# Taking the gathered rows of u at an even pace, earlier, with a higher claim on VectorE

## The chip, the cores and the metric

One core of a Trainium2 chip runs the whole program. The metric is the device time of one execution in microseconds (us). Before the change the median of three runs is 2525.91 us (2525.65 to 2526.83).

## The reference, cut to what matters

Two transformer blocks over 512 tokens of width 1024. The change touches only the last part of the second block, a mixture of 16384 tiny experts (`peer`):

```python
q = (h @ w_pq)...                       # 8 heads, two halves of the key
sc = einsum("bshcd,hcnd->bshcn", q, sub_keys)
s_top, i_top = lax.top_k(sc, 16)        # best 16 of 128 sub-keys, per half
cand = s_top[..., 0, :, None] + s_top[..., 1, None, :]
best, pos = lax.top_k(cand, 16)         # best 16 of 256 pairs
expert_idx = ...                        # 8 x 16 = 128 experts per token
gate = softmax(best)
a = gelu(einsum("ced,cd->ce", u_emb[idx], hx))
out = einsum("ce,ced->cd", gate * a, v_emb[idx])
```

Each token needs 128 rows of `u_emb` (a dot product with the token's h) and 128 rows of `v_emb` (a weighted sum), each row 1024 floats.

## The kernel before, in words

**Two ways for the experts.** The 512 tokens lie in four blocks of 128. Tokens of blocks 1 to 3 (384) are computed densely: h times all 16384 columns of u on TensorE, then times a gate matrix that is zero for experts not chosen, then times all of v. Tokens of block 0 are computed by gathering: for each of their 128 expert slots an indirect DMA fetches one row of u per token into a 128 x 1024 tile (row n of the 128 u rows), and VectorE multiplies it with h and sums (`tensor_tensor_reduce`, in the profile `CUSTOM_DVE_ANT_0`) into column n of `ea`. After all 128, the 128 rows of v follow, each added to `yt` with its weight. This makes 256 row steps (`row_step`, `rows[0]` counts them). Their gathers are issued from GpSimd's queue (L1045). There are four row buffers (`NROW`), `row0`, `row1` and the ends of two larger tiles, which the profile calls `last`; the gather into a buffer waits until VectorE is done with the row in it.

**The stages.** (1) `peer_u` computes the queries and the heads' lists of best sub-keys (`head_lists`). (2) It computes the dense u products in 16 octets of 8; each of these 128 `linear` calls is 24 matmuls of 128 x 384. Beside them run the routing of each block (`block_best`: best pairs, expert numbers, softmax; almost all on VectorE) and then `gates`, which builds the gate matrices: for each group of 8 tokens VectorE makes five `hot` tiles, and TensorE multiplies them in 24 small bf16 matmuls (`gp`). The results go to DRAM (`g_dr`), as do 14 of the 16 octets of activations (`a_dr`). (3) The last stage runs 128 steps (`for i in range(NV - NLAST)` and its end): per step VectorE multiplies activation and gate (`wv`), ScalarE and VectorE split it into a high and a low part, and TensorE does 24 matmuls (`acc`). Every eight steps the next octet of gates (`goct`) and of activations comes back from DRAM, 1.5 MB each.

**Weights** of u and v stream in as pairs of units (`feed`, `raw`); each unit is split into a high part by ScalarE (`w..h`) and a low part (`w..l`) by VectorE or, while `gates_on` is false in the u products, by GpSimd. The split runs two units ahead of its use.

**The order of the work** is written by a planner at build time, and each engine then runs its instructions in that order. `Clock` holds a planned time for each engine: `Clock.cost` prices a VectorE instruction at 0.07 us and a nanosecond or so per element, a matmul at (at least 256) columns / 2400 us. `Merge` runs a main generator, here `peer_u`, and beside it side generators in lanes (`ls` for lists, routing and gates, one after the other; `rw` for rows). Each side generator yields when it wants to go on; whenever the main one yields, every side generator whose time is not past TensorE's planned time goes on, the smallest time first, and with equal times the one started first. A yield of `room("V", slack)` means: VectorE's planned time less `slack`, so a generator with a larger slack may pile more work on VectorE ahead of TensorE and goes first. `block_best` uses 1.5, the hots of `gates` 2.0, and the gate matmuls wait until 2.5 us (`GLAG`) after their hots. `u_rows`, the generator of the change, is started at the end of block 0's routing. It ends when 128 rows are done; what it hasn't done by the end of `peer_u` is done in the last stage, where `quota` spreads all rows that are left over the steps.

Of the kernel before, what the change touches and what calls it, by code (L numbers as in the profile page):

```python
# [41 lines left out]
TD = T - P  # L42
NTC = TD // TC
WAHEAD = 2
NRES = 2
VORD = list(range(NOCT - 1, NOCT - 1 - NRES, -1)) + list(range(NOCT - NRES))

# [15 lines left out]
class Clock:  # L63
# [53 lines left out]
    def room(self, kind, slack, *aps):  # L117

        return lambda: max(self.free[kind] - slack, self.at(*aps) if aps else 0.0)
# [70 lines left out]
def body(tc, a):  # L190
    nc = tc.nc
    clk = Clock()
    V, S, G, PE = (Engine(clk, k, e) for k, e in (("V", nc.vector), ("S", nc.scalar), ("G", nc.gpsimd),
                                                  ("PE", nc.tensor)))
    at, room = clk.at, clk.room
    with ExitStack() as ctx:
# [841 lines left out]
        def row_buf(n):  # L1038
            return bufs_[n % NROW]

        def fetch_row(upto):
            while fetched[0] < min(upto, 2 * P):
                n = fetched[0]
                t = a["vn"] if n >= P else a["un"]
                nc.gpsimd.indirect_dma_start(row_buf(n), None, t,  # L1045
                                             bass.IndirectOffsetOnAxis(ap=eid[:, n % P:n % P + 1], axis=0))
                start = max(clk.free["G"], at(row_buf(n), eid))
                clk.free["G"] = start + 1.2
                clk.put(row_buf(n), start + 5.0)
                fetched[0] += 1  # L1050

        rows = [0]

        def row_step():


            n = rows[0]
            rows[0] += 1
            fetch_row(n + NROW)
            r, e = row_buf(n), ea[:, n % P:n % P + 1]  # L1060
            if n < P:
                V.tensor_tensor_reduce(r, r, h2t[0], 1.0, 0.0, ALU.mult, ALU.add, e)
            elif n == P:
                V.tensor_scalar(yts[0], r, e, None, ALU.mult)
            else:
                V.scalar_tensor_tensor(yts[0], r, e, yts[0], ALU.mult, ALU.add)
            if n == P - 1:
                S.activation(ea, ea, AF.Gelu)
                V.tensor_tensor(ea, ea, eg, ALU.mult)

        def u_rows():
            while rows[0] < P:
                fetch_row(rows[0] + NROW)
                yield room("V", 0.3, row_buf(rows[0]))
                row_step()
        iota = wk.tile([P, P], F32, name="iota")
        G.iota(iota, pattern=[[1, P]], base=0, channel_multiplier=0, allow_small_or_imprecise_dtypes=True)
        iota2 = wk.tile([P, P, 2], BF16, name="iota2")
# [50 lines left out]
        def block_best(b):  # L1129
# [48 lines left out]
            if b == 0:  # L1178
                V.scalar_tensor_tensor(eid, IJG[:, 0, 0], float(P), IJG[:, 0, 1], ALU.mult, ALU.add)
                V.tensor_copy(eg, IJG[:, 0, 2])  # L1180
                mg.spawn("rw", u_rows())
            yield room("V", 1.5)

        g_dr = dr.tile([NOCT, P, NTC, 8, TC], F32, name="g_dr")
        a_dr = [dr.tile([P, 8, TD], F32, name=f"a_dr{o}") for o in range(NOCT - NRES)]

# [59 lines left out]
        def peer_u():  # L1246
# [24 lines left out]
            for o in range(NOCT):  # L1271
                ao = acts[o % 2]
                if o >= NOCT - NRES:
                    aocts[o] = ao
                for j in range(8):
# [3 lines left out]
                    if o == NOCT - 1 and j == 7:  # L1279
                        for i in range(WAHEAD):  # L1280
                            list(weighted(i))
                    r = yield from linear(h2, f"u{o}{j}")
                    S.activation(ao[:, j], r[:, P:], AF.Gelu)
                if o < NOCT - NRES:
                    nc.scalar.dma_start(a_dr[o], ao)
# [31 lines left out]
        def weighted(i):  # L1317

            n, j = divmod(i, 8)
            ao, go = aocts[VORD[n]], octs[n]  # L1320
            w, h, l = t2(f"wv{i}"), t2(f"wv{i}h", F32R), t2(f"wv{i}l", F32R)
            d = slice(P, T)
            V.tensor_tensor(w[:, d].rearrange("p (c t) -> p c t", c=NTC),
                            ao[:, j].rearrange("p (c t) -> p c t", c=NTC), go[:, :, j, :], ALU.mult)
            S.activation(h[:, d], w[:, d], AF.Copy)
            yield
            V.tensor_tensor(l[:, d], w[:, d], h[:, d].bitcast(F32), ALU.subtract)
            if i == 0:
                S.activation(l[:, :P], ident, AF.Copy, scale=0.0)
            if j == 7:  # L1330
                del octs[n]
            ready[i] = h, l
# [9 lines left out]
        def mix(m, q, first, last):  # L1342

            wh, wl, vh, vl = q
            c = slice(m * P, (m + 1) * P)
            d = slice(P, T)
            e = slice(0, T) if first else d
            PE.matmul(acc8[m][:, e], vh[:, c], wl[:, e], start=first, stop=False)
            PE.matmul(acc8[m][:, d], vl[:, c], wh[:, d], start=False, stop=False)
            PE.matmul(acc8[m][:, d], vh[:, c], wh[:, d], start=False, stop=last)  # L1350
# [4 lines left out]
        for i in range(NV - NLAST):  # L1355
# [4 lines left out]
            quota = min(2 * P, row0 + 4 + i * (2 * P - row0) // (NV - 12))  # L1360
            w = weighted(i + WAHEAD)
            next(w)
# [6 lines left out]
            for m in range(KT):  # L1369
                mix(m, q, i == 0, False)  # L1370
        for i in range(NV - NLAST + WAHEAD, NV):
            list(weighted(i))
# [150 lines left out]
```

## Time and profile before

| | |
|---|---|
| median of three runs | 2525.91 us |
| profiled execution | 2525.12 us, its span 2523.4 us |
| TensorE (PE) busy | 2404.9 us, 95% |
| VectorE (DVE) busy | 1774.1 us, 70% |
| ScalarE (ACT) busy | 1022.2 us, 41% |
| GpSimd (POOL) busy | 747.6 us, 30% |
| DMA | 466.13 MB, mean 185 GB/s |
| mean granted clock of TensorE | 0.978 |

Busy times come from the hardware profiler and can overlap between engines. A wait names the engine or transfer that released it. A busy TensorE is not TensorE at its peak. Times in the tables count from the span's start.

### The profile page before, as it was taken

To read this page: it belongs to the slowest core of one execution; us is meant where nothing else is said; L and a number is where in the kernel's file an instruction comes from. 1 tells how busy PE (TensorE), PEld (TensorE's weight loads), DVE (VectorE), ACT (ScalarE), POOL (GpSimd) and SP (SyncE) were. 2 spreads that over 40 slices of the span, in tenths; PEclk is the share of its full clock that TensorE was granted. 3 is DMA by queue.
4 is the path that set the end of the run, shared out by engine and by line. 5 is a ranking of instruction groups with operands and counts; after the bars stand their busy time and mean duration, and the time that the engine had idled before them with its cause. 6 is when DMAs were issued, how large, how long until landed. Compare 5 with 4: busy or idle time off the path is not lost.

```text
span 2523.4 us, 33808 instructions
## 1 busy us (share of the span) xinstructions
PE 2404.9 (95%) x13113; PEld 2135.8 (85%) x13121; DVE 1774.1 (70%) x3172; ACT 1022.2 (41%) x1558; POOL 747.6 (30%) x581
## 2 busy tenths in 40 slices
PE   9999999999999999999999999999998988898987
PEld 7777888888776668888899999999998988898887
DVE  4647644433468888556799999975577878787885
ACT  4454423322355665533233457653332323232333
POOL 2122011100137767003252300022234434444431
PEclk9999999999999999999999999999999999899998
DMA  4110222222211112222245568888889998999982
GB/s 164 57 51 34 105 100 85 99 101 100 84 51 51 51 51 100 85 99 92 91 155 189 184 219 266 270 303 300 305 305 373 331 368 334 371 337 361 358 322 90
DMA packets 128896, 466.13 MB, mean 185 GB/s; under 512 B 9184, under 2 KB 60512, under 8 KB 95200
## 3 DMA queue, kind: packets, MB, share of 16 engines
q1 hardware_dynamic: 39456, 281.04, 30.4%
q0 software_dynamic: 36864, 134.23, 14.7%
q10 hardware_dynamic: 52416, 48.70, 5.8%
q8 instruction: 103, 1.69, 0.3%
q14 instruction: 57, 0.47, 0.1%
HBM read 414.65 MB, written 49.28 MB: 184 GB/s over the span
## 4 chain that ended last, share of the span: by engine, by line
PE 44%; issue 25%; DVE 11%; DMA 10%; POOL 7%; ACT 3%; POOLq 0%; DVEq 0%; SPq 0%; ACTq 0%
PE u L133 8%; PE up L133 5%; DMA last<-in_vn,eid 5%; PE gate L133 5%; DMA row<-in_vn,eid 4%; PE pq L133 3%; POOL last L1045 3%; POOL row L1045 3%; PE acc L133 2%; PE wo L133 2%; DVE yt L133 2%; PE qkb L133 2%; PE ao L133 2%; PE gc L133 2%; PE co L133 2%
## 5 line engine op out<-in xcount | busy, mean ns | idle before, releaser
L133 POOL TENSOR_TENSOR cy<-cy,cvt 128x511 f32<-128x511 f32 (+14 forms) x120 | 170.7, 1422 | 59.2 <-ACT cvt L133 42.9
L1045 POOL DMA_INDIRECT last<-in_un,eid x64 | 74.0, 1156 | 342.2 <-DVE ea L133 317.4
L133 ACT ACTIVATE last<-u 128x384 f32<-128x384 f32 x128 | 63.4, 495 | 251.8 <-PE u L133 251.6
L1045 POOL DMA_INDIRECT last<-in_vn,eid x64 | 88.8, 1388 | 103.4 <-DVE yt L133 95.3
L1045 POOL DMA_INDIRECT row<-in_vn,eid x64 | 87.1, 1360 | 106.5 <-DVE yt L133 96.1
L1045 POOL DMA_INDIRECT row<-in_un,eid x64 | 75.7, 1183 | 123.4 <-DVE ea L133 120.7
L133 ACT ACTIVATE stage<-gp 128x512 f32<-128x512 f32 x96 | 95.9, 1106 | 36.7 <-PE gp L133 20.4
L133 DVE SCALAR_TENSOR_TENSOR yt<-row,ea,yt 128x1024 f32<-128x1024 f32 x64 | 82.1, 1283 | 37.1 <-DMA row<-in_vn,eid 37.1
L133 DVE SCALAR_TENSOR_TENSOR yt<-last,ea,yt 128x1024 f32<-128x1024 f32 x63 | 80.8, 1283 | 38.1 <-DMA last<-in_vn,eid 38.0
L133 DVE TENSOR_TENSOR hot<-hot,ijb 128x1024 bf16<-128x1024 bf16 x144 | 91.4, 687 | 1.6
L133 DVE SCALAR_TENSOR_TENSOR cyp<-u,par,cyp 128x511 f32<-128x511 f32 (+28 forms) x116 | 85.4, 736 | 2.4
L133 ACT ACTIVATE cvt<-u,par 128x511 f32<-128x511 f32 (+14 forms) x120 | 78.6, 701 | 0.7 <-DVE u L133 0.7
L133 PEld LDWEIGHTS <-hot 128*128 128x128 bf16 x1152 | 66.4, 97 | 13.1 <-DVE hot L133 8.5
L133 PE MATMUL gp<-hot,hot 128*128 128x128 bf16 x1152 | 74.7, 219 | 2.7 <-DVE hot L133 2.6
L133 DVE TENSOR_TENSOR wv<-last,goct 128x384 f32<-128x384 f32 x128 | 70.9, 554 | 0.0
L133 DVE TENSOR_TENSOR hot<-iota,ijb 128x1024 bf16<-128x1024 bf16 x96 | 61.8, 686 | 0.1
L133 DVE CUSTOM_DVE_ANT_0 last<-last,h2s 128x1024 f32<-128x1024 f32 x34 | 41.6, 1223 | 23.8 <-DMA last<-in_un,eid 23.8
L133 DVE CUSTOM_DVE_ANT_0 row<-row,h2s 128x1024 f32<-128x1024 f32 x36 | 44.0, 1223 | 12.5 <-DMA row<-in_un,eid 12.5
L133 DVE TENSOR_TENSOR su<-up,n2r 128x512 f32<-128x512 f32 x22 | 15.2, 691 | 51.7 <-PE up L133 51.7
L133 DVE MAX8 stop__8676<-skc 128x8 f32<-128x128 f32 x128 | 36.8, 287 | 5.5 <-ACT skc L133 3.2
L133 PEld LDWEIGHTS o<-v,pT 128*128 128x128 f32 x224 | 27.8, 191 | 14.8 <-ACT pT L133 7.6
L133 DVE CUSTOM_DVE_ANT_0 last<-last,h2tok 128x1024 f32<-128x1024 f32 x30 | 36.5, 1216 | 5.1 <-DMA last<-in_un,eid 5.1
(6461 smaller groups left out, 8606.2 us busy)
## 6 DMA issues: line engine op xcount, KB each, us to landing
raw<-in_w SPq DMA_DIRECT2D x89, 1024.0 KB, 4.8
raw<-in_u SPq DMA_DIRECT2D x64, 1024.0 KB, 6.4
raw<-in_v SPq DMA_DIRECT2D x64, 1024.0 KB, 7.7
g_dr<-stage ACTq DMA_DIRECT2D x24, 1024.0 KB, 7.0
goct<-g_dr SPq DMA_DIRECT2D x16, 1536.0 KB, 12.5
a_dr<-last ACTq DMA_DIRECT2D x14, 1536.0 KB, 10.0
last<-a_dr SPq DMA_DIRECT2D x14, 1536.0 KB, 17.3
xT<-in_x_t SPq DMA_DIRECT2D x1, 1024.0 KB, 9.5
```

Source lines behind the costliest of these rows:

```text
L133: return f(*args, **kw)
L1045: nc.gpsimd.indirect_dma_start(row_buf(n), None, t, bass.IndirectOffsetOnAxis(ap=eid[:, n % P:n % P + 1], axis=0))
```

## The change

`u_rows` asks for VectorE with a slack of 1.5 us instead of 0.3, and after each row it yields a time `due`, 3.5 us of planned time after the one before (`PACE`), so that rows come evenly. If it falls behind, it may be at most two paces late, and then catches up. The gather of the row four ahead, which was issued right after a row step, is now issued when the next row is due.

```diff
+PACE = 3.5
...
         def u_rows():
+
+            due = clk.free["PE"]
             while rows[0] < P:
                 fetch_row(rows[0] + NROW)
-                yield room("V", 0.3, row_buf(rows[0]))
+                yield room("V", 1.5, row_buf(rows[0]))
+                due = max(due + PACE, clk.free["PE"] - 2 * PACE)
                 row_step()
+                yield due
```

## Rows read from the trace of the kernel before

**Rows 1.** Busy time of each engine by stage; (x) counts instructions.

```profile
core 0: us, PE busy (x) PEld busy (x) DVE busy (x) ACT busy (x) POOL busy (x), PEclk, DMA share, GB/s
1350.00:1469.00 119.00, 116.78 (x666) 116.43 (x665) 108.90 (x330) 49.77 (x67) 36.49 (x17) 0.99 0.52 195
1469.00:1667.00 198.00, 195.28 (x1863) 184.94 (x1862) 195.51 (x296) 136.36 (x159) 12.05 (x12) 1.00 0.80 249
1667.00:1865.60 198.60, 197.73 (x1140) 197.09 (x1139) 114.82 (x149) 70.76 (x99) 49.46 (x49) 1.00 0.87 318
1865.60:2478.90 613.30, 544.49 (x2929) 533.97 (x2930) 492.10 (x634) 181.43 (x246) 259.85 (x192) 0.94 0.90 341
```

**Rows 2.** Timeline of TensorE in the last stage: start, duration, instruction, idle before.

```profile
1870.32 0.33 PE L133 MATMUL acc<-wv1l,w309h 128*128 128x384 f32 x1
...
2170.17 0.34 PE L133 MATMUL acc<-wv60l,w368h 128*128 128x384 f32 x1
...
2174.33 0.34 PE L133 MATMUL acc<-wv61l,w369h 128*128 128x384 f32 x1
...
2199.72 0.69 PE L133 MATMUL acc<-wv66h,w374l 128*128 128x384 f32 x1 [4.26 <-DVE w374l L133]
...
2206.53 0.34 PE L133 MATMUL acc<-wv67l,w375h 128*128 128x384 f32 x1
...
2478.86 0.34 PE L133 MATMUL acc<-wv122l,w430h 128*128 128x384 f32 x1
```

**Rows 3.** After a long and a short wait of TensorE: clock, and the short wait.

```profile
2199.72:2205.33 5.61, 5.61 (x17) 5.61 (x18) 3.80 (x6) 1.86 (x3) 1.77 (x2) 0.50 0.97 375
2101.80:2106.00 4.20, 4.19 (x24) 4.19 (x25) 4.20 (x6) 1.95 (x4) 1.77 (x2) 1.00 0.72 263
...
2101.81 0.45 PE L133 MATMUL acc<-wv47h,w355l 128*128 128x384 f32 x1 [1.45 <-DVE w355l L133]
```

**Rows 4.** Waits of VectorE in the last stage: total us, times, longest.

```profile
DVE yt L133 <- DMA last<-in_vn,eid: 38.0, 20, 4.0
DVE yt L133 <- DMA row<-in_vn,eid: 37.1, 22, 4.6
DVE last L133 <- DMA last<-in_un,eid: 23.8, 12, 3.9
DVE row L133 <- DMA row<-in_un,eid: 12.5, 9, 3.3
```

**Rows 5.** Groups of VectorE in the last stage: steps on rows of u.

```profile
L133 DVE CUSTOM_DVE_ANT_0 last<-last,h2s 128x1024 f32<-128x1024 f32 x34 | 41.6, 1223 | 23.8 <-DMA last<-in_un,eid 23.8
L133 DVE CUSTOM_DVE_ANT_0 row<-row,h2s 128x1024 f32<-128x1024 f32 x34 | 41.5, 1223 | 12.5 <-DMA row<-in_un,eid 12.5
```

**Rows 6.** Timeline of GpSimd in routing: weight splits, one block apart.

```profile
1390.73 2.40 POOL L133 TENSOR_TENSOR w214l<-raw,w214h 128x1024 fp32r<-128x1024 f32 x1 [20.61 <-ACT w214h L133]
...
1427.60 2.39 POOL L133 TENSOR_TENSOR w223l<-raw,w223h 128x1024 fp32r<-128x1024 f32 x1 [22.10 <-ACT w223h L133]
```

**Rows 7.** Timeline of VectorE in the gates: two weight splits, two rows of u.

```profile
1502.60 1.22 DVE L133 TENSOR_TENSOR w238l<-raw,w238h 128x1024 fp32r<-128x1024 f32 x1
...
1510.01 1.22 DVE L133 TENSOR_TENSOR w239l<-raw,w239h 128x1024 fp32r<-128x1024 f32 x1
...
1529.09 1.22 DVE L133 CUSTOM_DVE_ANT_0 last<-last,h2tok 128x1024 f32<-128x1024 f32 x1
...
1530.23 1.22 DVE L133 CUSTOM_DVE_ANT_0 row<-row,h2tok 128x1024 f32<-128x1024 f32 x1
```

**Rows 8.** DMA of the last stage: bytes moved, and median us to landing.

```profile
DMA packets 40536, 209.33 MB, mean 341 GB/s; under 512 B 4511, under 2 KB 4511, under 8 KB 29091
...
row<-in_vn,eid POOLq DMA_INDIRECT x64, 8.4
```

**Rows 9.** Timeline of TensorE in the gates: one group's small matmuls.

```profile
1503.14 1.56 PE L133 MATMUL gp<-hot,hot 128*128 128x128 bf16 x24
1504.51 0.42 PE L133 MATMUL u<-h2l,w236h 128*128 128x384 f32 x1
```

## The prediction

> **What bounds the kernel now.** I read the table by stage first, then the waits of VectorE and the matmul timeline in the last stage, then the timeline of one gate cycle.
>
> The change touches what follows 1350 us, where the first block's routing ends. Four stages follow [rows 1]: routing of blocks 1 to 3 (119 us), the gates (198 us), the rest of the u products (198.6 us) and the last stage, the v products (613.3 us). In routing TensorE is the bound: VectorE is busy 108.9 us of 119. In the gates both are full, VectorE a little more: 195.5 of 198 us. In the rest of the u products TensorE has no gap and VectorE is busy 114.8 of 198.6 us. In the last stage the granted clock is 0.94, the DMA share 0.90, and TensorE stands idle 69 us.
>
> One step of the last stage (24 matmuls for one product) takes 2174.33 − 2170.17 = 4.16 us undisturbed [rows 2]. From step 1 (1870.32) to step 122 (2478.86) are 608.5 us for 121 steps; at 4.16 they would be 503.4. So 105 us are lost. The loss comes in lumps: in step 66 TensorE waits 4.26 us for the split of weights w374, and step 67 starts 7.0 us after that wait ended, not 4.16 us, because most of the matmuls after it ran at a clock of 0.50, the lower level (1.2 GHz) [rows 2, 3]. VectorE itself had been standing before a row that had not landed: 111.4 us of such waits in the stage, for rows of v and of u [rows 4]. So the bound there is the transfer of rows. 68 of the 128 u rows are left to this stage [rows 5], on top of 128 v rows.
>
> **The change, part by part.** It adds and removes no instruction; it moves row steps, each with its gather on GpSimd's queue, from the last stage into the three before. So the sum has a gain behind 1865.6 us and a cost before.
>
> *How many rows move.* The claim on VectorE goes from 0.3 to 1.5 us ahead of TensorE in the planner's time, and a row is due each 3.5 us of it. I walked the planner's rules by hand. In its prices a linear is 24 × 384/2400 = 3.84 us, a split or a row 1.14, a hot 0.60.
>
> Routing: routing has the claim 1.5 as well, and rows win a tie, since they were spawned before the next block's steps. A block now takes nine linears (w214 to w223 on GpSimd, 36.9 us) [rows 6], 34.6 us in the plan; at 3.5 us that is 10 rows. VectorE's plan is then full, and a block grows to about ten linears. So 30 rows for three blocks, where there is 1 now.
>
> Gates: the pattern repeats after two groups of 8 tokens and one linear, 7.41 us (1502.60 to 1510.01 by the weight splits) [rows 7]. In the plan it is 2 × 2.56 + 3.84 = 8.96 us, since 128-column matmuls are priced as 256 columns. The hots' claim (2.0) beats the rows' (1.5): a row gets in only when a group's five hots are all placed and the gates wait for their 2.5 us of lag. Followed through a cycle this happens once; the wait for the lag then is shorter, but the cycle in the plan stays 8.96 us, because the row fits where VectorE's plan had a hole before the next split. So 24 rows in 24 cycles, far under the pace, and about 11 between the gate blocks as now.
>
> After the gates: about one row per linear now; at 3.5 us, 3.84/3.5 = 1.1 per linear. With about 44 linears left, some 49 rows.
>
> Sum: 30 + 24 + 11 + 49 = 114 rows done before the last stage, against 60 now: 54 move, and 14 remain.
>
> *The gain in the last stage.* A row is 128 × 4 KB = 0.524 MB, so 54 are 28.3 MB of the 209.3 MB that the stage moves at 341 GB/s [rows 8]. At that rate: 83 us. Ceiling: the 105 us of lost time, since below 4.16 us per step TensorE is the bound; that would need (209.3 − 28.3) MB in 508 us, 356 GB/s, somewhat more than the mean now. Floor: half the lumps stay because they come with the octets' transfers, which the change leaves, 40 us. I take 80, next to the rate: the ring of four row buffers speaks for it. At 196/116 = 1.69 rows per step three rows ahead are 3/1.69 × 4.16 = 7.4 us of lead, less than the median landing of 8.4 us [rows 8]; at 142/116 = 1.22 they are 10.2 us.
>
> *The cost before.* A row takes 1530.23 − 1529.09 = 1.14 us of VectorE [rows 7].
>
> In a gate cycle VectorE has no room: the row makes 7.41 into 8.55 us. TensorE needs 2 × 1.37 us for the gate matmuls (1503.14 to 1504.51) and 4.16 for the linear, 6.9 us [rows 9], so it is VectorE that sets the length, and TensorE waits for hots 1.65 us of each cycle instead of 0.5. 24 × 1.14 = 27 us.
>
> In routing 29 rows more are 33 us, and the extra splits about 2 us; the 10 us that VectorE is idle there now shrink to some 4, as it falls behind. VectorE's own work to the end of the gates is 108.9 + 195.5 + 33 + 27 + 2 + 4 = 370 us after 1350, against 317 now: 53 us later. TensorE does three more linears in this time, 3 × 4.16 = 12.5 us that it doesn't have to do behind it. Cost: 41 us. After the gates a linear leaves VectorE over 1.5 us free even with a split and 1.1 rows (1.14 + 1.25 of 4.16), so nothing is added there.
>
> What the cost hides behind: TensorE's other linears, which the plan puts in front of the hots; that cover is short because the plan prices the gate matmuls at nearly twice their time and so takes VectorE for free where it is full. From below, with 20 rows in routing and five more linears: 50 − 10 − 21 = 19 us. From above, with two rows in each gate cycle: 41 + 27 = 68 us.
>
> GpSimd's queue: while its half of the splits runs there, a gather that waits for VectorE's last use of the buffer stands ahead of a weight split of 2.39 us, and TensorE waits for that. The gathers are paced, 3.5 us after the row, and the split is needed two linears (8.3 us) later; I count nothing, at most 15 us. Landing of rows in routing and gates: three rows ahead are over 10 us there; nothing.
>
> Sum against the profiled execution (2525.1 us, span 2523.4): −80 + 41 = −39, 2486 us. The median shown is 0.8 us above that execution: 2487 us.
>
> A rule against it: waits of TensorE cost twice when the clock falls. Here a wait of 1.45 us at 2101.81 left the clock at 1.00, one of 4.26 us brought 0.50 [rows 3]. The waits that I add are under 1 us each, so I count none. The Trainium skill ("TensorE: Matmul & The Clock Gate", section "A second HAM failure mode: psum-queue depth-cycling") says that TensorE's many small idles between groups of matmuls can make its clock go back and forth. By that, the gates would go as in rival B; the gates now, with 0.5 us of idle per cycle at a clock of 1.00 [rows 1, 9], neither show nor exclude it.
>
> **The rivals.**
>
> A: the last stage keeps half its lumps. Each octet's two transfers of 1.57 MB share the queues with the rows whatever their number. For it: the lumps come once per eight steps. Against it: the waits are for rows, and the stage moves near its best rate throughout. Gain 40, cost 41: 2526 us, no change.
>
> B: the clock falls in the gates. If TensorE's waits of about 0.8 us per group bring the lower level, a matmul of 384 columns takes 5.61 us/17 = 0.33 us instead of 0.173 [rows 3], a cycle 6.9 × 1.85 = 12.8 us at that level alone. TensorE is then the bound and has no waits, so the level comes back; half the cycles at either gives (12.8 + 8.55)/2 = 10.7, and 24 × 2.1 = 51 us: 2538 us, slower. It decides where its price passes the 39 us of the sum, at some 1.6 us per cycle, a mean clock of about 0.75 between 1469 us and the end of the gates.
>
> C: the cost is near its lower end (19 us) as VectorE's lag in routing is taken up by the slack of the planner's order, and the gain as summed: 2465 us. For it: TensorE hardly waits in routing now. Against: the gates are full.
>
> D: the rows don't get in, as the gates' claim stays ahead and what is due isn't forced: 2526 us. Against: routing and the time after the gates have room by the same rules.
>
> **How the numbers follow.** Forecast 0.62, A 0.13, B 0.07, C 0.15, D 0.03. Around the forecast's 2487 the counts of rows and the rate leave ±25. The range 2450 to 2524 holds the forecast and C; above lie B and half of A, below the case where cost is 19 and gain over 95. A change of 0.2% (5 us) can be told: faster is the forecast, C, and a third of A, 0.82; same a third of A and D, 0.07; slower B and a third of A, 0.11.
>
> **What would show it.** Right: the gate cycle at about 8.5 us by the weight splits with one row in it, and the gates ending near 1720 us; some 114 rows before the first v product, which starts near 1906 us; steps of the last stage at 4.3 to 4.4 us on average, and VectorE's waits for rows at well under half of 111 us. Wrong: lumps of 7 us still at each octet; a clock under 0.95 in the gates; the first v product later than 1930 us; under 90 rows done by it.

## The result, and the profile after

The changed kernel takes 2459.28 us (median of four runs, 2453.93 to 2461.22) against 2526.37 us: a ratio of 0.973 (95% interval 0.9712 to 0.9747), 67 us faster where 39 were forecast. Its profiled execution has a span of 2459.2 us, 64.2 less than before, and the parts below are of that pair.

The stages of the changed kernel, cut at the end of block 0's routing, the last routing, the last gate matmul, the first v product and step 122. Columns are as in [rows 1], whose second and third cuts lie some 6 and 2 us behind the last routing and the last gate matmul:

```profile
1354.10:1554.90 200.80, 198.57 (x1147) 198.22 (x1146) 183.60 (x449) 78.49 (x105) 107.29 (x74) 1.00 0.86 316
1554.90:1793.00 238.10, 205.90 (x1910) 194.53 (x1909) 224.51 (x344) 141.77 (x165) 48.52 (x35) 0.99 0.86 273
1793.00:1901.60 108.60, 107.00 (x617) 106.36 (x615) 68.67 (x94) 39.94 (x56) 36.89 (x33) 1.00 0.92 338
1901.60:2414.90 513.30, 509.96 (x2928) 507.40 (x2929) 425.72 (x518) 184.25 (x246) 158.27 (x134) 1.00 0.90 350
```

The last stage went from 613.3 to 513.3 us, and its clock from 0.94 to 1.00. The first v product comes at 1901.6 instead of 1865.6 us, 36.0 later. The end after step 122 is 44.3 us as it was 44.5. So −100.0 + 36.0 − 0.2 = −64.2. Of the 36 us, 4.6 were there before the first row, in code that the change doesn't touch. The VectorE timeline of the kernel before, then of the changed one, at the instruction that makes the row numbers:

```profile
1349.67 0.29 DVE L133 SCALAR_TENSOR_TENSOR eid<-IJG 128x128 int32<-128x128 f32 x1
```

```profile
1354.27 0.28 DVE L134 SCALAR_TENSOR_TENSOR eid<-IJG 128x128 int32<-128x128 f32 x1
```

That leaves 31 us of cost to the change. Nearly all of it stands in one line of TensorE's waits (total us, times, longest): first the kernel before, from 1350 to 1866 us, then the changed one, from 1354 to 1902 us:

```profile
PE gp L133 <- DVE hot L133: 2.6, 15, 0.2
```

```profile
PE gp L134 <- DVE hot L134: 32.2, 25, 2.8
```

The gate cycle is where it comes from. VectorE's timeline in the changed kernel, two weight splits one cycle apart, with the row between:

```profile
1606.31 1.22 DVE L134 TENSOR_TENSOR w260l<-raw,w260h 128x1024 fp32r<-128x1024 f32 x1
...
1613.72 1.21 DVE L134 CUSTOM_DVE_ANT_0 row<-row,h2tok 128x1024 f32<-128x1024 f32 x1
...
1614.86 1.22 DVE L134 TENSOR_TENSOR w261l<-raw,w261h 128x1024 fp32r<-128x1024 f32 x1
```

8.55 us, where it was 7.41 [rows 7], and one row in it: both as forecast.

TensorE's timeline in the last stage at steps 1 and 122:

```profile
1906.33 0.33 PE L134 MATMUL acc<-wv1l,w309h 128*128 128x384 f32 x1
...
2414.91 0.34 PE L134 MATMUL acc<-wv122l,w430h 128*128 128x384 f32 x1
```

508.6 us for 121 steps: 5.2 us above 121 × 4.16, where 105 were lost [rows 2]. VectorE still waits for rows in this stage, 44.8 us for rows of v and 0.5 us for rows of u instead of 111.4 in all [rows 4], but TensorE hardly feels it: its own waits there are 3.4 us. The longest wait of VectorE is 3.2 us now, where it was 4.6:

```profile
DVE yt L134 <- DMA row<-in_vn,eid: 23.8, 17, 3.2
DVE yt L134 <- DMA last<-in_vn,eid: 21.0, 16, 2.8
```

The groups of VectorE's steps on rows of u by the copy of h that they read (`h2tok` until the last stage is set up near the end of the u products, `h2s` after) tell how many were left: 14, where the kernel before has 34 + 34 of them in the last stage [rows 5] and 2 just ahead of it. Of the 14, four come ahead of the first v product. So 118 rows are done by then, where it was 60, and 10 are left to the stage.

```profile
L134 DVE CUSTOM_DVE_ANT_0 last<-last,h2tok 128x1024 f32<-128x1024 f32 x58 | 70.1, 1214 | 12.0 <-DMA last<-in_un,eid 12.0
L134 DVE CUSTOM_DVE_ANT_0 row<-row,h2tok 128x1024 f32<-128x1024 f32 x56 | 67.6, 1215 | 10.7 <-DMA row<-in_un,eid 10.6
L134 DVE CUSTOM_DVE_ANT_0 row<-row,h2s 128x1024 f32<-128x1024 f32 x8 | 9.8, 1219 | 0.5 <-DMA row<-in_un,eid 0.5
L134 DVE CUSTOM_DVE_ANT_0 last<-last,h2s 128x1024 f32<-128x1024 f32 x6 | 7.2, 1220 | 0.0
```

The stage's DMA line of the changed kernel [rows 8]:

```profile
DMA packets 32419, 179.78 MB, mean 350 GB/s; under 512 B 3606, under 2 KB 3606, under 8 KB 20978
```

Bytes fell by 29.6 MB (28.3 forecast), and the rate went up from 341 to 350 GB/s. At 341 the stage could have gained 87 us; it gained 100.

### The profile page after: what moved, and what is told of

The parts are those of the page before. It is cut to its first block, busy times and chain, and to the rows that moved or that the text cites. A ratio compares the mean times of both kernels' runs of the same rounds, so it can differ in the third digit from the quotient of the medians.

```text
span 2459.2 us, 33812 instructions
## 1 busy us (share of the span) xinstructions
PE 2377.5 (97%) x13113; PEld 2114.3 (86%) x13121; DVE 1766.6 (72%) x3167; ACT 1028.8 (42%) x1558; POOL 740.3 (30%) x586
## 4 chain that ended last, share of the span: by engine, by line
PE 56%; issue 16%; DVE 13%; DMA 8%; POOL 3%; ACT 3%; ACTq 0%; DVEq 0%; SPq 0%; POOLq 0%
PE u L134 14%; PE acc L134 7%; PE up L134 5%; PE gate L134 5%; PE pq L134 3%; DMA row<-in_vn,eid 3%; DMA raw<-in_v 2%; DVE yt L134 2%; PE wo L134 2%; DMA last<-in_vn,eid 2%; PE qkb L134 2%; PE ao L134 2%; PE co L134 2%; PE gc L134 2%; DVE m L134 1%
## 5 line engine op out<-in xcount | busy, mean ns | idle before, releaser
L1046 POOL DMA_INDIRECT last<-in_un,eid x64 | 81.6, 1274 | 200.2 <-DVE ea L134 166.3
L1046 POOL DMA_INDIRECT row<-in_vn,eid x64 | 75.2, 1175 | 158.7 <-DVE yt L134 150.1
L1046 POOL DMA_INDIRECT last<-in_vn,eid x64 | 74.1, 1158 | 146.4 <-DVE yt L134 137.6
L134 ACT ACTIVATE stage<-gp 128x512 f32<-128x512 f32 x96 | 95.6, 1105 | 44.8 <-PE gp L134 42.2
L134 DVE CUSTOM_DVE_ANT_0 last<-last,h2tok 128x1024 f32<-128x1024 f32 x58 | 70.1, 1214 | 12.0 <-DMA last<-in_un,eid 12.0
L134 DVE CUSTOM_DVE_ANT_0 row<-row,h2tok 128x1024 f32<-128x1024 f32 x56 | 67.6, 1215 | 10.7 <-DMA row<-in_un,eid 10.6
```

Of the source, the lines that this page charges most:

```text
L134: return f(*args, **kw)
L1046: nc.gpsimd.indirect_dma_start(row_buf(n), None, t, bass.IndirectOffsetOnAxis(ap=eid[:, n % P:n % P + 1], axis=0))
```

## The experiments

Four questions: is it the bytes or the lead of the gathers that held the last stage; is the cost where I put it; which half of the change does the work; and what is left.

**A deeper ring alone.** The kernel before; from the last stage on, four more row buffers from the space that is free there.

```diff
+        more, sw, depth = [], [4 * P], [NROW]
...
         def row_buf(n):
-            return bufs_[n % NROW]
+            j = (n - sw[0]) % 8
+            return bufs_[n % NROW] if n < sw[0] else more[j] if j < 4 else bufs_[(sw[0] + j) % NROW]
...
-            fetch_row(n + NROW)
+            fetch_row(n + depth[0])
...
+            more.extend(wk.tile([P, D], F32, name=f"more{i}") for i in range(4))
+            sw[0], depth[0] = fetched[0], 8
```

> The kernel before, with eight row buffers instead of four from the start of the last stage on; nothing else moves, 68 u rows stay in that stage. Theory R (rate): the stage is bound by the bytes it moves, 209 MB at 341 GB/s; then the deeper ring gives under 15 us. Theory L (lead): the stage is bound by how far ahead of its use a row's gather starts, three rows or 7.4 us at full pace, less than the 8.4 us of a median landing; with seven rows ahead (17 us) the lumps at each octet shrink, and 40 us or more of the 105 lost ones come back (2485 us or less).

Measured: 2462.73 us, ratio 0.9747 (0.9731 to 0.9764). As much as the change, with every row left where it was. The stage from step 1 to step 122, and then ScalarE's waits in it:

```profile
1870.08:2412.74 542.66, 519.99 (x2905) 511.92 (x2905) 482.93 (x625) 181.97 (x244) 251.09 (x187) 0.98 0.96 380
```

```profile
ACT w344h L133 <- DMA raw<-in_v: 7.2, 1, 7.2
ACT w360h L133 <- DMA raw<-in_v: 6.7, 1, 6.7
ACT w376h L133 <- DMA raw<-in_v: 5.4, 1, 5.4
```

The same queues move 380 GB/s with seven rows in flight, where three gave 341. So 341 was not what the memory gives but what four buffers let through: theory L. Of the 105 us, 39 stay lost, and VectorE no longer waits for rows; ScalarE waits for weights of v, 61.6 us in all, a new wait in the old one's place. A part of it reaches TensorE, which waits 14.8 us for the high parts that ScalarE makes.

**Half of the rows.** The changed kernel, `while rows[0] < 87` in `u_rows`.

> The changed kernel, but its early rows end at 87 of 128, so that 27 more (half of those that moved) are left to the last stage, 1.46 rows per step. Theory R: 27 x 0.524 MB = 14.2 MB more at 350 GB/s, 40 us more than the changed kernel, about 2500 us. Theory L: the lead is 8.6 us, over the median landing but under the long ones; a few lumps come back, 10 to 25 us more, 2470 to 2484 us.

Measured: 2496.34 us (0.9889, 0.9869 to 0.9908), 37 us over the changed kernel. This is R's number and not L's, though the run above excludes R as it stood, a stage bound by its bytes at 341 GB/s. What fits both runs is a throughput that four buffers allow: each row then has a price, even where the lead is longer than the median landing. The lost time from step 1 to 122 (over 503.4 us), by the number of u rows that read `h2s`, of this run and the two below: 70 rows (before) 105 us, 51 rows 62, 41 rows (this run) 45, 40 rows 37, 14 rows 5. From end to end 100 us for 56 rows, 1.8 us each on average, somewhat above the 0.524 MB at 341 GB/s (1.54 us) by which I had counted. The price isn't even: 1.2 us a row from 14 to 40, 2.3 us from 51 to 70. Of the 100 us, 65 are waits of TensorE (68.8 us idle before, 3.3 in the changed kernel), and the rest went with the longer matmuls at the lower clock (0.94 before, 1.00 after).

**The old claim in the gates alone.** In the changed kernel a flag that `gates` sets and clears:

```diff
-                yield room("V", 1.5, row_buf(rows[0]))
+                yield room("V", 0.3 if in_gates[0] else 1.5, row_buf(rows[0]))
```

> The changed kernel, but while the gate matrices are built the rows ask with the old claim of 0.3 us instead of 1.5. My account of the cost (24 rows at 1.14 us on a full VectorE, seen as 32 us of TensorE's waits for hots): the gate cycle goes back from 8.55 to 7.41 us and TensorE's waits for hots to under 8 us, so the v products begin 25 to 30 us sooner. The price: some 24 rows go to the last stage (1.4 per step). R: 36 us more there, in all 2465 us; L: 10 to 20 us more, in all 2440 to 2450 us. A rival on the cost, that the late start of the v products comes from routing, expects no earlier start.

Measured: 2461.90 us (0.9744, 0.9727 to 0.9761), no different from the changed kernel. TensorE's waits for hots in its profile, and its gate stage (the last routing to the last gate matmul):

```profile
PE gp L134 <- DVE hot L134: 7.3, 16, 1.9
```

```profile
1553.70:1759.00 205.30, 197.71 (x1876) 187.28 (x1875) 193.88 (x290) 137.34 (x161) 9.44 (x8) 1.00 0.77 247
```

The first v product comes at 1870.4 us, 31 sooner; counted from `eid` it is 28.5 us, out of 31 of cost. Routing is still as long as in the changed kernel. So nearly all of the cost is the gates', and the rival (routing) falls. The last stage loses 37 us, 32 more than in the changed kernel: close to R's 36, not L's 10 to 20. What the gates saved, the 26 rows that were left to the last stage cost again.

**The right price for the gate matmuls.** In the planner, for the changed kernel:

```diff
-        return max(n, 256) / 2400 if ins[-1].dtype != F32 else 0.03 + n / 600
+        return max(n, 128 if ins[-1].dtype == BF16 else 256) / 2400 if ins[-1].dtype != F32 else 0.03 + n / 600
```

> The changed kernel, but the planner prices the bf16 matmuls of 128 columns at 128 instead of 256 columns, which is near what they take (1.37 us for 24). My account: VectorE is then full in the plan too, more linears come between the gate matmuls, and TensorE's waits for hots go from 32 to under 10 us; 20 to 27 us faster than the changed kernel, 2432 to 2440 us. If the waits have another reason than the price, under 5 us change.

Measured: 2479.37 us (0.9815, 0.9798 to 0.9831): 20 us slower than the changed kernel, where I expected 20 to 27 faster. The mechanism held, and the sum did not. No wait for hots is left; the gate stage of this run:

```profile
1553.40:1804.50 251.10, 251.10 (x2201) 243.55 (x2200) 218.24 (x315) 157.25 (x188) 16.50 (x14) 1.00 0.77 252
```

TensorE is busy throughout, and the first v product comes at 1861.1 us, 40 sooner (39 counted from `eid`). But with an honest plan VectorE has no room for rows: 13 get in during the gates instead of 33, and with fewer linears left behind them 51 read the second copy of h, 47 of them in the last stage, which loses 62 us. I had forgotten that the wrong price was also what let the rows in.

**Claim and pace apart.** The claim alone (the `due` lines taken out), and the pace alone (0.3 instead of 1.5).

> The higher claim alone: u_rows asks with 1.5 us, but without due times, so a row may go as soon as VectorE's claim allows and its transfer has landed in the plan. If the claim does the work: all 128 rows are done before or early in the gates, the gate cycle stays near 7.41 us, the v products start sooner than in the changed kernel (1902 us), by up to 30 us, and the last stage keeps its 4.16 us per step: 2425 to 2450 us. Rival: without the pace the rows, which win ties, push routing and gates so late that the last gates run behind the u products and TensorE stands still for them: over 2470 us.

> The pace alone: due times as in the change, but the old claim of 0.3 us. If the claim does the work, the rows stay out of routing and gates as before, some 60 are done before the last stage, and the time is that of the kernel before, within 8 us. If the pace does it, at least half of the 64 us that the change gave.

The claim alone: 2466.94 us (0.9762, 0.9746 to 0.9779). The pace alone: 2528.23 us against 2525.28 (1.0013, 1.0003 to 1.0023): nothing gained, no rows up to the last routing, 12 in the gate stage, 60 in all before the last stage, as in the kernel before. So the claim does the work. Without the pace the rows push routing back, and neither number that I gave comes out: routing takes 279 us (84 rows in it), the gates still take about one row per cycle (37 with the gaps between blocks), since it is the hots' claim and not the pace that limits them there, and all rows are done before the last stage, which loses 0.4 us. The first v product comes at 1917 us, 15 later than in the changed kernel (18 counted from `eid`). The pace is worth some 8 us (2459 against 2467 us), with intervals of the ratios that just touch (0.9712 to 0.9747 and 0.9746 to 0.9779).

**The deeper ring on top.** The two kernels without waits for hots, each with the eight buffers.

> The kernel with the old claim during the gates (88 rows before the last stage, v products from 1870 us, 37 us lost in the last stage), and eight row buffers in the last stage. Theory L: the 37 us were the ring's; under 8 us stay, 2430 to 2438 us. Theory R, now at the 387 GB/s that the deeper ring reached: (128 + 40) rows are 182 + 14 = 196 MB, 506 us, no more than TensorE's own 508, so the same number; below 8 us stay. If the rows aren't what holds the stage but the weights' transfers, 20 us or more stay, 2445 us and up.

> The kernel with the gate matmuls priced at 128 columns (no waits for hots, v products from 1860 us, 77 rows before the last stage, 62 us lost there), and eight row buffers in the last stage. L and R at 387 GB/s: 182 + 19 = 201 MB take 519 us, 11 us over TensorE's 508; with the sooner start 2428 to 2440 us. If it were the rows' number alone, whatever the ring, 60 us would stay lost, 2475 us.

Measured: 2441.97 us (0.9661, 0.9644 to 0.9677) and 2435.51 us (0.9650, 0.9631 to 0.9669). In the profiled executions the ring takes back 14 us of the lost 37 and 39 of the 62, and in both 23 us stay, with ScalarE waiting up to 7.7 us for weights (`ACT <- DMA raw`). So the first was missed: it lies between the two numbers that I gave. The second is in its range, though I had counted 11 us there. The profiled execution of the first was its slowest, 9 us over the median, so less than 23 us may be usual in it. Whether the bytes, which differ by 11 rows, matter here isn't shown by this pair.

**The octets in quarters.** SyncE's queue holds the v weights behind two transfers of 1.57 MB at each octet. Each octet of activations is now fetched in four pieces, one per step:

```diff
-        def fetch_a(n):
-            if n < NOCT and VORD[n] not in aocts:
+        def fetch_a(n, q):
+            if n < NOCT and (q or VORD[n] not in aocts) and VORD[n] < NOCT - NRES:
                 aocts[VORD[n]] = acts[(n + 1) % 2]
-                nc.sync.dma_start(aocts[VORD[n]], a_dr[VORD[n]])
+                h = slice(2 * q, 2 * q + 2)
+                nc.sync.dma_start(aocts[VORD[n]][:, h], a_dr[VORD[n]][:, h])
...
-                fetch_a(i // 8 + 1)
+            if 1 <= i % 8 <= 4:
+                fetch_a(i // 8 + 1, i % 8 - 1)
```

> The changed kernel with the gate matmuls priced at 128 columns, eight row buffers in the last stage, and each octet of activations fetched in four quarters of 0.39 MB, one per step, instead of one transfer of 1.57 MB. What was left there (23 us) showed as ScalarE's waits for the v weights, which stand behind the octet on SyncE's queue. If the order of transfers is the cause, under 10 us stay: 2413 to 2424 us. If it is the bytes (376 GB/s), the spread changes under 5 us: 2430 to 2440 us.

> The kernel before with only the eight row buffers and the octets in quarters; the 68 u rows stay in the last stage, which needs 209 MB in 509 us, 411 GB/s, to run at TensorE's pace. If bytes bound it (380 GB/s with the deeper ring alone), it stays within 10 us of the deeper ring alone, 2453 to 2465 us, and moving rows early is worth some 25 us on its own account; if the order of transfers was all, 20 us or more come back, 2443 us or less, and the early rows are worth little more than a deeper ring.

Measured: 2414.59 us, ratio 0.9561 (0.9548 to 0.9574), and 2439.76 us, 0.9659 (0.9645 to 0.9672). The last stage of the first, then of the second:

```profile
1857.80:2370.00 512.20, 511.47 (x2948) 510.83 (x2948) 469.86 (x595) 194.79 (x249) 223.48 (x167) 1.00 0.97 389
```

```profile
1870.00:2400.00 530.00, 516.41 (x2944) 510.64 (x2943) 489.41 (x632) 183.93 (x247) 254.83 (x188) 1.00 0.98 393
```

The first loses 0.0 us from step 1 to 122: from the gates to step 122 TensorE has one wait, of 0.7 us at the first v product. So the way in which the octets were fetched was the cause of the last 23 us; whether it was the size of the pieces or their later start, the edit doesn't separate. It is the fastest kernel here, 112 us faster than the one before. The second, with no row moved, gets 23 us by the same edit, which is the number that I had given for the order of the transfers, and still loses 20 us, at 393 GB/s and a DMA share of 0.98. The GB/s in 40 slices from 1870 to 2400 us, in the kernel before and in the second:

```profile
GB/s 304 287 400 360 330 404 333 315 369 359 324 352 382 316 357 411 287 339 416 290 358 417 309 329 416 333 341 417 304 305 394 357 300 398 350 310 384 396 318 393
```

```profile
GB/s 323 375 412 412 420 409 406 419 407 416 412 412 415 410 411 417 408 414 413 413 415 410 410 419 406 414 412 412 416 413 408 417 408 412 411 411 398 273 160 158
```

What came in bursts before now flows at 398 to 420 GB/s for 460 us. At 4.16 us a step, a unit of weights, an eighth of two octets and 196/116 rows would need some 430 GB/s by my estimate, the first kernel with 47 + 128 = 175 rows in the stage 410. So here bytes are the likely bound. Beside a good ring, moving rows early, with the right price for the gate matmuls, is worth 25 us (2439.76 − 2414.59), not 67. What the change is worth there without that price, no run shows.

## Why the prediction was right, point by point

**What bounds the kernel.** Right that the last stage was held by rows that hadn't landed. That this is a matter of the ring rather than of the rate, the prediction named as support and not as the reason; the deeper ring showed it to be the reason for 66 of the 105 us.

**How many rows move.** 114 forecast before the first v product, 118 measured: 58 rows moved, not 54. The sum came near by compensation, though. By stage, counted in VectorE's timeline: routing 53 (30 forecast), gates 33 (35 forecast), after the gates 32 up to 1901.6 us (49 forecast). The step that failed is "a block grows to about ten linears": blocks grew to sixteen (48 weight splits on VectorE and GpSimd from 1354 to 1555 us, 27 before), and with them the rows, 53 in 48 linears, which is the 1.1 per linear of the pace. VectorE's timeline in routing shows why (start, duration, instruction), first in the kernel before:

```profile
1406.97 1.23 DVE L133 TENSOR_TENSOR w218l<-raw,w218h 128x1024 fp32r<-128x1024 f32 x1 [0.73 <-ACT w218h L133]
1408.11 0.69 DVE L133 TENSOR_TENSOR eq<-pab,iota 128x1024 bf16<-128x1024 bf16 x1
...
1411.28 1.22 DVE L133 TENSOR_TENSOR w219l<-raw,w219h 128x1024 fp32r<-128x1024 f32 x1
1412.41 0.69 DVE L133 TENSOR_TENSOR eq<-pab,iota 128x1024 bf16<-128x1024 bf16 x1
```

Then in the changed one:

```profile
1409.57 1.22 DVE L134 TENSOR_TENSOR w217l<-raw,w217h 128x1024 fp32r<-128x1024 f32 x1
1410.71 1.21 DVE L134 CUSTOM_DVE_ANT_0 row<-row,h2tok 128x1024 f32<-128x1024 f32 x1
...
1411.85 0.69 DVE L134 TENSOR_TENSOR eq<-pab,iota 128x1024 bf16<-128x1024 bf16 x1
...
1415.02 1.22 DVE L134 TENSOR_TENSOR w218l<-raw,w218h 128x1024 fp32r<-128x1024 f32 x1
1416.15 1.21 DVE L134 CUSTOM_DVE_ANT_0 row<-row,h2tok 128x1024 f32<-128x1024 f32 x1
...
1417.29 1.22 DVE L134 TENSOR_TENSOR w219l<-raw,w219h 128x1024 fp32r<-128x1024 f32 x1
1418.43 1.21 DVE L134 CUSTOM_DVE_ANT_0 last<-last,h2tok 128x1024 f32<-128x1024 f32 x1
...
1419.57 0.69 DVE L134 TENSOR_TENSOR eq<-pab,iota 128x1024 bf16<-128x1024 bf16 x1
```

Each linear brings a split and a row, and a step of routing (`eq`) gets in only at every second one (w217, w219, not w218), where the kernel before has one at each. I had let the rows lengthen the block once, and had not followed how each further linear brings a further row and a further split.

**The cost.** 41 forecast, 31 measured. The gates' part came out as counted (27 forecast; TensorE's waits for hots rose by 29.6 us). Routing's part, 53 − 27 − 12.5 = 13.5 us in the sum, is the term that was too large: TensorE is busy 198.6 of routing's 200.8 us. VectorE's part was larger than counted: some 52 rows more, not 29, and 31 weight splits instead of 15, some 18 us where I had 2. But because the blocks grew to sixteen linears, TensorE had enough to do, and the longer routing was paid for by a shorter stage after the gates (108.6 instead of 198.6 us). So the mechanism that I used for the lower bound, more linears beside routing, ran further than in that bound: 21 more, not five. The gates ended at 1792.5 us, not near 1720 as forecast, and the first v product came close to the 1906 us of the forecast all the same.

**The gain.** 80 forecast, 100 measured, near the ceiling of 105. The term mis-sized is 54 rows at the rate of 341 GB/s. What stood in its place is 1.8 us per row moved away from a ring of four, and an end to the long waits behind which the clock fell: it is at 1.00 in the stage now. The argument from the lead (7.4 us against a landing of 8.4; 10.2 after) pointed at the ring, which was right, but gave no better number: two runs with more rows left lost 40 and 32 us more where it said 10 to 25 and 10 to 20. Gain and cost were missed to the same side, so the time came 28 us under the forecast, 9 us inside the lower end of the range.

**The rivals.** A (lumps stay with the octets): fell; 5.2 us are lost in the stage. But the octets do hold up the weights in the runs with the deeper ring, until they are fetched in quarters. B (clock in the gates): fell; the clock over the stage is 0.99. The waits were longer than the "under 1 us each" of the prediction, mostly 1.3 us, one per cycle, and two were near 2.8. TensorE's clock behind these two (the columns of [rows 1]), then the two waits:

```profile
1576.54:1579.40 2.86, 2.86 (x25) 2.86 (x26) 2.83 (x5) 2.23 (x4) 0.00 (x0) 0.50 0.94 268
1629.34:1630.90 1.56, 1.56 (x25) 1.56 (x26) 1.52 (x3) 1.56 (x3) 0.00 (x0) 1.00 0.93 348
```

```profile
1576.54 2.74 PE L134 MATMUL gp<-hot,hot 128*128 128x128 bf16 x24 [2.72 <-DVE hot L134]
...
1629.34 1.55 PE L134 MATMUL gp<-hot,hot 128*128 128x128 bf16 x24 [2.83 <-DVE hot L134]
```

So B's mechanism came once, behind the wait of 2.72 us, and cost some 1.6 us by my estimate (24 gate matmuls took 2.50 us instead of 1.37, and three behind them 1.03 instead of 0.52), where B needed 39. The Trainium skill ("TensorE: Matmul & The Clock Gate", section "A second HAM failure mode: psum-queue depth-cycling") tells of a kernel in which many small idles between groups of matmuls made the clock go back and forth. Such idles are here too, about one in each cycle, and the clock left its upper level once in 238 us: this trace doesn't agree. C: its reason, that VectorE's lag in routing is taken up, is what came, and its 2465 us is the nearest total; but its cost of 19 us is no nearer to the 31 measured than the forecast's 41, and it had the gain at 80. D fell.

## What to carry to other kernels

When a stage is short of gathered rows, look at how many are in flight before counting its bytes: a ring of four gave 341 GB/s and looked like a bandwidth bound, and a ring of eight on the same traffic gave 380. A claim in a planner is paid where the planner's price for something else is wrong; mending that price alone made things slower here, since the slack that it invented was where the moved work fitted. So mend the price and the ring together, and then see which transfer the next wait stands behind.

## What the runs showed of the hardware that I had not expected

Two queues of this core, weights and octets on one and gathered rows on the other, sustained 393 GB/s over 530 us at a DMA share of 0.98; the highest mean of a slice of 63 us in the kernel before was 373. And the length of a wait alone doesn't tell what TensorE's clock does behind it: of 25 waits in 238 us, one of 2.72 us had matmuls at 0.50 behind it, one of 2.83 us had them at 1.00, and the others, up to 1.7 us, left the clock at 1.00, while one of 4.3 us was followed by 5.6 us at 0.50 [rows 3].
